# Moving the sixteen tiles of one operand set by 32 bytes each in a two-layer encoder kernel

## The chip, the cores and the metric

The kernel runs on one core of a Trainium2 chip. The metric is the device time of one execution in microseconds, taken over several executions. One further execution was recorded by the hardware profiler; all durations below come from it.

## The reference

The reference is an encoder of two layers on 512 tokens of width 1024, in float32. Layer 0 mixes tokens by dilated sliding-window attention (16 heads, three groups of windows), layer 1 by differential attention (8 heads with two softmaxes each, and a norm on each head's result). Each mixer is followed by a squared-ReLU MLP with 4096 hidden units. Cut to what matters:

```python
for i in range(2):
    hn = rms_norm(h, norm_mix_g[i])
    mix = dilated_window_attention(hn, ...) if i == 0 else differential_attention(hn, ...)
    h = h + mix
    h = h + sq_relu_mlp(rms_norm(h, norm_mlp_g[i]), mlp_w_in[i], mlp_w_out[i])
return rms_norm(h, norm_final_g)

def sq_relu_mlp(xn, w_in, w_out):
    u = jax.nn.relu(xn @ w_in)
    return (u * u) @ w_out
```

## The kernel before, in words

Activations lie transposed: the residual is eight tiles `hT[0..7]` of 128 features by 512 tokens, 2048 bytes in each partition. TensorE multiplies in a short float32 form (`F32R`), so every operand is split into a high part and a low remainder, and every product is three matmuls. The helper `mm3` (L168) issues them in this order: weights high with activations high (L169), weights high with activations low (L170), weights low with activations high (L171).

A matmul here has a stationary operand, loaded by its own instruction (LDWEIGHTS, engine PEld in the profile), and a moving operand that is streamed through. In `linear_steps` (L173) the weights are stationary, 128 columns at a time, and a set of activation tiles is moving, 512 tokens wide. For one block of 128 output features it runs over eight tiles `k` of the set, three matmuls each, so 24 matmuls that accumulate in one PSUM tile. Only in `values1` (L739) it is the other way: there the activations are stationary in slices of 128 tokens, and the weights move, 256 columns wide. The records write a matmul as out<-moving,stationary.

A set of activation tiles is made by `xset` (L128): eight tiles for the high parts and eight for the low parts, each 128 x 512 of four bytes. There are three kinds:

- Set A holds the normed residual. `Norm.feed` (L228) writes a tile of it with one ScalarE instruction (L232, `Ah`) and one VectorE instruction (L233, `Al`). It is the moving operand of all q, k and v products of layer 0, of the q and k products of layer 1 and of all first MLP products, and the stationary operand of `values1`. The norms of both layers, before mixer and MLP, use the same sixteen places in turn.
- Set B (tags `Bh`, `Bl`) holds MLP hidden units; its places also serve for attention operands, and as `oh`, `ol` for the input of the output projections.
- Set C (tags `Ch`, `Cl`, made in `m_in`, not by `xset`) holds the other half of the hidden units.

Weights come in units of 1 MB (`fetch`, L140) through two buffers of three tiles each: `raw`, `whi`, `wlo`, 8192 bytes per partition. ScalarE makes the high part (L158), VectorE the low part (L159).

The order on TensorE is the order in which the program issues, with a few steps woven in (`woven`, L209; hooks in `linear_steps`). Nothing in it depends on where a tile lies.

Where the tiles lie: pools are laid out one behind the other in each partition, in steps of 32 bytes, in the order `const`, `hpool` (the residual, set A, set B), `rpool`, `wpool` (weights), `spool`, and then the pools of a stage. Within `hpool` the order is `h0` to `h7`, `Ah0` to `Ah7`, `Al0` to `Al7`, then the places of set B. In the program before, `Ah0` begins at byte 33888 of each partition, `Al7` at 64608, the first place of set B at 66656, the first `whi` at 121952 and the first `wlo` at 138336. In what follows the **phase** of an operand is its first byte modulo 512. A column block of weights is 128 columns of four bytes, so 512 bytes; a change of `k` or of the block moves it by 1024 or 512 bytes and leaves its phase. The phases before:

| operand | first byte | phase |
|---|---|---|
| `Ah0` to `Al7` | 33888 + 2048 n | 96 |
| set B and its other uses (`oh`, `ol`, `k`, `o`, `pt`) | 66656 + 2048 n | 96 |
| set C, `qh`, `ql`, `nacc`, `h` | various | 96 |
| `whi`, `wlo` | 121952 and on | 96 |
| `ptn`, `psg`, `v0` (layer 0), `p` (layer 1) | 193312 and on | 288 |
| `aT` (layer 1) | 221152, 223200 | 480 |
| `on` (layer 1) | 226336 | 32 |
| `ident` (moving operand of transposes) | 16512 | 128 |

Of the kernel before, what the change touches and what calls it, by code (L numbers as in the profile page):

```python
# [12 lines left out]
F32R = mybir.dt.float32r  # L13
# [6 lines left out]
P = 128  # L20
SEQ = 512
DM = 1024
DFF = 4096
KT = DM // P
# [57 lines left out]
def tile_encoder(ctx: ExitStack, tc: tile.TileContext, x, rel_bias, gains, norm_final_g,  # L82
# [5 lines left out]
    hpool = ctx.enter_context(tc.tile_pool(name="hpool", bufs=1))  # L88
# [37 lines left out]
    hT = [hpool.tile([P, SEQ], F32, tag=f"h{d}", name=f"h{d}") for d in range(KT)]  # L126

    def xset(tag):  # L128
        return ([hpool.tile([P, SEQ], F32R, tag=f"{tag}h{d}", name=f"{tag}h{d}") for d in range(KT)],
                [hpool.tile([P, SEQ], F32R, tag=f"{tag}l{d}", name=f"{tag}l{d}") for d in range(KT)])  # L130

# [86 lines left out]
    class Norm:  # L220


        def __init__(self, gcol, tag):
            self.gcol = gcol
            self.xs = xset(tag) if tag else None
            self.acc = spool.tile([P, SEQ], F32, tag="nacc", name="nacc", bufs=1)
# [368 lines left out]
    for p in range(8):  # L595
        f = sN[:, :, 2 * p:2 * p + 2] if p < 3 else sS[:, :, 2 * p - 6:2 * p - 4]
# [30 lines left out]
    def mlp(i, nm, nxt, last=False):  # L627
# [5 lines left out]
        def m_in(c):  # L633
            if c % 2 == 0:
                hs = xset("B")
            else:
                hs = ([mp.tile([P, SEQ], F32R, tag=f"Ch{d}", name=f"Ch{d}", bufs=1) for d in range(KT)],
                      [mp.tile([P, SEQ], F32R, tag=f"Cl{d}", name=f"Cl{d}", bufs=1) for d in range(KT)])
            chunks[c] = hs

            def on_out(d, ps):
                u = mp.tile([P, SEQ], F32, tag="u", name="u")
                nc.vector.scalar_tensor_tensor(u, ps, 0.0, nm.rB, op0=ALU.max, op1=ALU.mult)  # L643
                nc.scalar.activation(u, u, AF.Square)  # L644
                nc.scalar.copy(hs[0][d], u)
                nc.vector.tensor_sub(hs[1][d], u, f32(hs[0][d]))

            for q in range(4):
                run(linear_steps(2 * q, KT, 256, xs, on_out, bank=wide, hooks=nm.hooks() if c + q == 0 else ()))
# [297 lines left out]
```

## Time and profile before

| | |
|---|---|
| time, median of 3 runs | 1233.21 us (1232.64 to 1233.25) |
| the profiled execution's own time | 1232.82 us |
| its span, first to last instruction | 1231.0 us |
| mean granted TensorE clock | 0.993 |
| VectorE busy | 637.5 us (52%) |
| ScalarE busy | 499.3 us (41%) |
| GpSimd busy | 116.3 us (9%) |
| DMA | 115.73 MB, mean 94 GB/s |

How to read it: the span is what the profile covers, and 1.8 us of the execution's own time lie around it. PE is the matmul engine and PEld its weight loads, which ride beside the matmuls. A matmul's duration runs from its start to a modelled end behind the pipeline, so matmuls of one stream overlap in the records: a 128 x 512 matmul is shown with some 0.39 us, while the next one starts about 0.23 us after it. What a matmul costs is therefore read from the distance between starts; the durations serve to tell one matmul from another. A group row gives line, engine, operation, out<-in, shapes and count, then the busy time in us and the mean of one in ns, then the idle time ahead of it.

### The profile page before, as it was taken

The numbers are of one execution on the slowest core, as the hardware profiler recorded it, in microseconds if no ns is written. First come the engines' busy times: TensorE is split into PE (matmuls) and PEld (weight loads), VectorE is DVE, ScalarE is ACT, GpSimd is POOL, SyncE is SP. The second block draws the span as 40 slices with busy tenths as digits, with TensorE's granted clock in tenths as the row PEclk, the third lists the DMA queues.
The fourth block names the chain that finished last, engine by engine and source line by source line (L and its number), as shares of the span: only waits on it lengthen the run. The fifth ranks groups of instructions, "written<-read, shape, count | busy, mean of one in ns | idle before, by whom it ended". The sixth has DMA issues, their size and how long they took to land.

```text
span 1231.0 us, 15250 instructions
## 1 busy us (share of the span) xinstructions
PE 1206.0 (98%) x6096; PEld 1020.2 (83%) x6096; DVE 637.5 (52%) x1039; ACT 499.3 (41%) x905; POOL 116.3 (9%) x219
## 2 busy tenths in 40 slices
PE   7989999999999999999999999998999999999997
PEld 5778878888888888888888998986888888888897
DVE  7764455645433434434478677673754334344333
ACT  5452433434322323313357667653544223133133
POOL 5000000210000000000201232322300000000012
PEclk9989999999999999999999999998999999999999
DMA  7261222233223333223422333121333223332211
GB/s 226 72 123 56 69 69 69 69 103 103 87 86 102 103 103 102 82 90 103 147 81 87 99 124 104 65 85 52 103 103 102 78 95 103 103 103 99 80 62 69
DMA packets 108307, 115.73 MB, mean 94 GB/s; under 512 B 4507, under 2 KB 101915, under 8 KB 108187
## 3 DMA queue, kind: packets, MB, share of 16 engines
q1 hardware_dynamic: 108236, 114.75, 30.0%
q8 instruction: 48, 0.79, 0.3%
q14 instruction: 23, 0.19, 0.0%
HBM read 112.50 MB, written 2.24 MB: 93 GB/s over the span
## 4 chain that ended last, share of the span: by engine, by line
PE 94%; DVE 2%; DMA 2%; ACT 1%; POOL 0%; issue 0%; SPq 0%; POOLq 0%; DVEq 0%; ACTq 0%
PE acc L169 15%; PE acc L171 15%; PE acc L170 15%; PE s_ps L170 13%; PE s_ps L171 13%; PE s_ps L169 13%; PE o_ps L800 2%; PE s_ps L345 1%; PE s_ps L346 1%; PE t_ps L791 1%; DMA B<-fd 1%; PE o_ps L525 1%; PE s_ps L494 1%; PE o_ps L529 1%; PE t_ps L485 0%; DMA h<-in_x_dram 0%
## 5 line engine op out<-in xcount | busy, mean ns | idle before, releaser
L158 ACT CAST whi<-raw 128x1024 fp32r<-128x1024 f32 (+1 forms) x194 | 192.7, 1039 | 392.8 <-PE s_ps L170 217.1
L159 DVE TENSOR_TENSOR wlo<-raw,whi 128x1024 fp32r<-128x1024 f32 (+1 forms) x194 | 233.7, 1241 | 22.9 <-ACT whi L158 22.5
L171 PE MATMUL acc<-Ah,wlo 128*128 128x512 f32 x472 | 185.9, 394 | 0.0
L169 PE MATMUL acc<-Ah,whi 128*128 128x512 f32 x472 | 185.8, 394 | 0.0
L170 PE MATMUL acc<-Al,whi 128*128 128x512 f32 x472 | 185.7, 393 | 0.0
L169 PE MATMUL s_ps<-Ah,whi 128*128 128x512 f32 x360 | 141.6, 394 | 5.7 <-ACT whi L158 5.5
L170 PE MATMUL s_ps<-Al,whi 128*128 128x512 f32 x360 | 142.1, 395 | 1.8 <-DVE Al L233 1.7
L171 PE MATMUL s_ps<-Ah,wlo 128*128 128x512 f32 x360 | 141.3, 393 | 0.0
L169 PEld LDWEIGHTS acc<-Ah,whi 128*128 128x128 f32 x472 | 89.0, 189 | 18.6 <-ACT sp L338 0.5
L171 PEld LDWEIGHTS acc<-Ah,wlo 128*128 128x128 f32 x472 | 88.8, 188 | 18.7 <-DVE wlo L159 0.5
L170 PEld LDWEIGHTS acc<-Al,whi 128*128 128x128 f32 x472 | 88.9, 188 | 18.1 <-issue 0.5
L169 PEld LDWEIGHTS s_ps<-Ah,whi 128*128 128x128 f32 x360 | 68.2, 190 | 20.3 <-ACT whi L158 5.5
L170 PEld LDWEIGHTS s_ps<-Al,whi 128*128 128x128 f32 x360 | 68.1, 189 | 17.6 <-DVE Al L233 3.8
L171 PEld LDWEIGHTS s_ps<-Ah,wlo 128*128 128x128 f32 x360 | 68.3, 190 | 14.2 <-DVE wlo L159 0.3
L644 ACT ACTIVATE u<-u 128x512 f32<-128x512 f32 x64 | 40.0, 628 | 96.6 <-DVE u L643 95.9
L250 POOL TENSOR_TENSOR nacc<-nacc,nsq 128x512 f32<-128x512 f32 x18 | 27.5, 1529 | 527.1 <-ACT nsq L248 526.6
L653 DVE TENSOR_TENSOR h<-h,s_ps 128x512 f32<-128x512 f32 x33 | 22.7, 688 | 105.4 <-PE s_ps L171 105.4
L643 DVE SCALAR_TENSOR_TENSOR u<-s_ps,rB 128x512 f32<-128x512 f32 x40 | 27.6, 691 | 83.8 <-PE s_ps L171 77.1
L775 DVE CUSTOM_DVE_ANT_0 p<-s_ps,bias 128x512 f32<-128x512 f32 x64 | 43.4, 688 | 31.0 <-PE s_ps L346 20.8
L171 PE MATMUL s_ps<-Bh,wlo 128*128 128x512 f32 x152 | 59.2, 389 | 0.0
L169 PE MATMUL s_ps<-Bh,whi 128*128 128x512 f32 x152 | 59.2, 389 | 0.0
L170 PE MATMUL s_ps<-Bl,whi 128*128 128x512 f32 x152 | 59.1, 389 | 0.0
(237 smaller groups left out, 2269.0 us busy)
## 6 DMA issues: line engine op xcount, KB each, us to landing
raw<-in_mlp_w_in_dram SPq DMA_DIRECT2D x32, 1024.0 KB, 5.3
raw<-in_mlp_w_out_dram SPq DMA_DIRECT2D x32, 1024.0 KB, 5.2
raw<-in_b_w_qkv_dram SPq DMA_DIRECT2D x12, 1024.0 KB, 5.2
raw<-in_a_w_qkv_dram SPq DMA_DIRECT2D x11, 1024.0 KB, 5.2
bias<-fd SPq DMA_DIRECT2D x16, 448.0 KB, 3.6
raw<-in_a_w_o_dram SPq DMA_DIRECT2D x4, 1024.0 KB, 5.2
raw<-in_b_w_o_dram SPq DMA_DIRECT2D x4, 1024.0 KB, 5.2
h<-in_x_dram SPq DMA_DIRECT2D x8, 256.0 KB, 5.1
```

The lines of the kernel that those rows point to most:

```text
L158: nc.scalar.copy(hi[:, k, c], raw[:, k, c])
L159: nc.vector.tensor_sub(lo[:, k, c], raw[:, k, c], f32(hi[:, k, c]))
L169: nc.tensor.matmul(ps, ahi, bhi, start=first, stop=False)
L170: nc.tensor.matmul(ps, ahi, blo, start=False, stop=False)
L171: nc.tensor.matmul(ps, alo, bhi, start=False, stop=last)
L250: eng.tensor_add(self.acc, self.acc, sq)
L345: nc.tensor.matmul(S, q[m][:, qs], k[m][:, ks], start=True, stop=False)
L643: nc.vector.scalar_tensor_tensor(u, ps, 0.0, nm.rB, op0=ALU.max, op1=ALU.mult)
L644: nc.scalar.activation(u, u, AF.Square)
L653: nc.vector.tensor_add(hT[ct], hT[ct], ps)
L775: nc.vector.tensor_tensor_reduce(out=xt, in0=S, in1=bias[h][m][:, b * P:b * P + SEQ], scale=1.0, scalar=3.0e38, op0=ALU.add, op1=ALU.min, ...
L800: marks["PV"] = nc.tensor.matmul(O[:, b, :], aT[:, k, :], v[:, k, es], start=k == 0, stop=k == NB - 1)
```

## The change

Each tile of set A is allocated with 520 columns in place of 512, and only its first 512 columns are handed on. A tile of set A so takes 2080 bytes of each partition, not 2048: `Ah0` stays where it is, each following tile lies 32 bytes further on than before relative to the one ahead of it, and everything behind set A moves by 16 x 32 = 512 bytes. Set B goes through the same helper with its old width. Instructions, their order, shapes and strides within a partition are those of before; only start addresses differ.

```diff
     def xset(tag):
-        return ([hpool.tile([P, SEQ], F32R, tag=f"{tag}h{d}", name=f"{tag}h{d}") for d in range(KT)],
-                [hpool.tile([P, SEQ], F32R, tag=f"{tag}l{d}", name=f"{tag}l{d}") for d in range(KT)])
+
+        n = SEQ + 8 if tag == "A" else SEQ
+        return tuple([hpool.tile([P, n], F32R, tag=f"{tag}{p}{d}", name=f"{tag}{p}{d}")[:, 0:SEQ] for d in range(KT)]
+                     for p in "hl")
```

## The prediction

> **What bounds the kernel now.** I read the page first: how busy each engine is, and who carries the chain of work that ended last.
>
> ```profile
> span 1231.0 us, 15250 instructions
> PE 1206.0 (98%) x6096; PEld 1020.2 (83%) x6096; DVE 637.5 (52%) x1039; ACT 499.3 (41%) x905; POOL 116.3 (9%) x219
> PE 94%; DVE 2%; DMA 2%; ACT 1%; POOL 0%; issue 0%; SPq 0%; POOLq 0%; DVEq 0%; ACTq 0%
> ```
>
> The reader is to see that the matmul engine is busy for 98% of the span and makes 94% of the chain. The table of stretches says the same of a single stage, here the MLP of layer 0 from 230 to 630 us:
>
> ```profile
> 230.00:630.00 400.00, 399.82 (x1787) 331.33 (x1786) 185.24 (x211) 139.21 (x183) 19.39 (x14) 1.00 0.32 101
> ```
>
> Of 400 us the matmul engine is busy for 399.82 (second figure), at the full granted clock (1.00), with VectorE at 185.24 and ScalarE at 139.21. So nothing else is late, and the time is the number of matmuls times the distance between their starts. The change touches neither number of instructions nor order; what it can touch is that distance. Next the groups of matmuls by operands:
>
> ```profile
> L171 PE MATMUL acc<-Ah,wlo 128*128 128x512 f32 x472 | 185.9, 394 | 0.0
> L171 PE MATMUL s_ps<-Ah,wlo 128*128 128x512 f32 x360 | 141.3, 393 | 0.0
> L169 PE MATMUL s_ps<-Bh,whi 128*128 128x512 f32 x152 | 59.2, 389 | 0.0
> L169 PE MATMUL acc<-whi,Ah 128*128 128x256 f32 x128 | 36.5, 285 | 0.0
> ```
>
> Each row has two sisters of the same count (L169, L170 and L171 are the three matmuls of a product). So set A is the moving operand of 3 x 472 + 3 x 360 = 2496 matmuls, and the stationary one of 3 x 128 = 384 narrower ones (last row). That A stands at 394 ns and B at 389 is no property of the tiles: it comes from where the A matmuls stand, as the timelines below show. In the middle of an MLP an A matmul is as quick as any:
>
> ```profile
> 306.04 0.39 PE L171 MATMUL acc<-Ah,wlo 128*128 128x512 f32 x1
> 306.27 0.39 PE L169 MATMUL acc<-Ah,whi 128*128 128x512 f32 x1
> ...
> 308.76 0.39 PE L171 MATMUL acc<-Ah,wlo 128*128 128x512 f32 x1
> 306.27 0.19 PEld L170 LDWEIGHTS acc<-Al,whi 128*128 128x128 f32 x1
> ```
>
> Twelve distances lie between 306.04 and 308.76: 2.72 / 12 = 226.7 ns each. The PEld row shows that the weights of the next matmul are loaded from the moment a matmul starts (306.27 both): the two read the same memory at the same time. That is where the phase could matter.
>
> **What the distance holds.** The granted clock is halved for a few microseconds near 74 us (0.50 in the row of the table of stretches, the last one here), and there 256-wide matmuls stand in a row:
>
> ```profile
> 73.21 0.41 PE L345 MATMUL s_ps<-sp,sp 128*128 128x256 f32 x1
> ...
> 74.28 0.41 PE L346 MATMUL s_ps<-sp,sp 128*128 128x256 f32 x1
> 73.20:74.30 1.10, 1.10 (x8) 1.10 (x7) 1.10 (x2) 1.10 (x4) 0.00 (x0) 0.50 0.72 126
> ```
>
> Five distances in 1.07 us: 214 ns for 256 columns, so 0.836 ns a column at half rate, and half of that, 0.418, at full rate. 512 columns then need 214 ns; the 226.7 ns hold 12.7 ns more, an extra which a slower matrix does not show. I take it for a cost of feeding two operands at once, and 12.7 ns as the most that a better position could give back per matmul. The TensorE page of the Trainium skill ("TensorE: Matmul & The Clock Gate", section "Wait — 56ns, not 53.3ns?") gives a warm matmul of 512 columns 215.7 ns from start to start, that is 2.5 ns of extra; the measured 226.7 ns decides here.
>
> The extra is not fixed. After a few 128-wide instructions the stream needs some ten matmuls to settle:
>
> ```profile
> 659.34 0.40 PE L170 MATMUL acc<-Al,whi 128*128 128x512 f32 x1
> ...
> 660.05 0.39 PE L170 MATMUL acc<-Al,whi 128*128 128x512 f32 x1
> 660.27 0.39 PE L171 MATMUL acc<-Ah,wlo 128*128 128x512 f32 x1
> ...
> 661.43 0.39 PE L170 MATMUL acc<-Al,whi 128*128 128x512 f32 x1
> ```
>
> Nine distances in 2.09 us: 232 ns on average, one of them (660.05 to 660.27) as short as 220 at this view's hundredth of a microsecond. After that the stream is at 227 again. So the distance depends on how the two reads stand against each other in time, settles as long as every matmul is like the last, and is 5.5 ns longer while it searches. How short the short one is, is told by the least of the durations in the view of the tile `Al` (least, median, most):
>
> ```profile
> L170 PE MATMUL acc<-Al,whi x472: 387/389/632, 14.9 to 1125.3; 128*128 128x512 f32 x158
> ```
>
> That is 2 ns under the median. With 256 columns the search goes the other way; in the last product, behind eight transposes:
>
> ```profile
> 1188.11 0.28 PE L170 MATMUL s_ps<-wlo,Ch 128*128 128x256 f32 x1
> ...
> 1188.93 0.28 PE L171 MATMUL s_ps<-whi,Cl 128*128 128x256 f32 x1
> 1189.06 0.28 PE L169 MATMUL s_ps<-whi,Ch 128*128 128x256 f32 x1
> ...
> 1190.26 0.28 PE L170 MATMUL s_ps<-wlo,Ch 128*128 128x256 f32 x1
> ```
>
> Seven distances in 0.82 us while it searches, 117 ns, and ten in 1.20 us when it has settled, 120 ns. A settled stream is not always the quickest.
>
> **Does the position in memory do the same?** Nearly all pairs of moving operand and weights in this kernel have the same phase (96), so the trace shows other phases only at the ends of streams, where the load beside the last matmul is of another tile. Below are rows of narrow windows, each with the last 512-wide matmul of a stream and the one whose operand is loaded beside it; ahead of each stand matmuls of 389 ns, so the stream had settled. First the load of `pt`, then that of `aT`:
>
> ```profile
> L169 PE MATMUL acc<-Ah,whi 128*128 128x512 f32 x1 | 0.4, 389 | 0.0
> L529 PE MATMUL o_ps<-vn,pt 128*128 128x64 f32 x1 | 0.2, 217 | 0.0
> ```
>
> ```profile
> L170 PE MATMUL acc<-Al,whi 128*128 128x512 f32 x1 | 0.4, 397 | 0.0
> L800 PE MATMUL o_ps<-v,aT 128*128 128x128 f32 x1 | 0.3, 274 | 0.0
> ```
>
> Two cases ahead of transposes, with `o` and with `p`:
>
> ```profile
> L169 PE MATMUL s_ps<-oh,whi 128*128 128x512 f32 x1 | 0.4, 393 | 0.0
> L600 PE MATMUL t_ps<-ident,o 128*128 128x128 f32 x1 | 0.3, 270 | 0.0
> ```
>
> ```profile
> L171 PE MATMUL acc<-Ah,wlo 128*128 128x512 f32 x1 | 0.4, 400 | 0.0
> L791 PE MATMUL t_ps<-ident,p 128*128 128x128 f32 x1 | 0.3, 273 | 0.0
> ```
>
> And one with `ptn`, at 106.0 us, ahead of L525:
>
> ```profile
> L169 PE MATMUL acc<-Ah,whi 128*128 128x512 f32 x1 | 0.4, 388 | 0.0
> ```
>
> With `pt` loading (phase 96, like the moving tile) the matmul keeps its 389 ns; with `aT` (phase 480, 384 further) it takes 397. Before transposes, whose load is of another kind, it is 393 with `o` (phase 96) and 400 with `p` (phase 288, 192 further). The last row is the exception: `ptn` is also 192 further, and the matmul stays at 388. So equal phase is the cheapest in both kinds, and another phase costs between 0 and 8 ns. That is thin (few phases, ends of streams), but it is the only evidence on position, and it speaks against the change.
>
> **The change part by part.** It adds and removes no instruction, wait or DMA.
>
> *The 2496 wide matmuls.* `Ah0` keeps its phase; tile n of the sixteen moves to 96 + 32 n, while the weights beside it stay at 96 (512 bytes further for all). So one tile in sixteen keeps the equal phase, and from one matmul to the next the difference jumps by 256 (from `Ah` to `Al` of one k) or by 32 more (to the next k): no matmul is like the last, and the stream may never settle. Bounds per matmul: 0 (the `ptn` row) and +8 ns (the `aT` row); below zero, the 2 ns of the shortest matmuls of the searching stream, and at the very most the 12.7 ns of the extra. I take +4 ns, the middle of 0 and 8, since the perpetual search would give 5.5 and one tile in sixteen pays nothing: 2496 x 4 ns = 10.0 us. All of it lies on the path, as the 399.82 of 400 us show.
>
> *The 384 narrow matmuls of `values1`.* There the weights move and slices of A are loaded, with the same differences. The nearest rows are the searching stream of that width, 3 ns under the settled one, and the wide rows, 0 to 8 ns over: so -1.2 to +3.1 us on 384. I take 0, which lies between, and keep both ends for the range.
>
> *Writing set A.* ScalarE and VectorE write the same 512 contiguous columns. The waits of the matmul engine for them:
>
> ```profile
> PE s_ps L170 <- DVE Al L233: 1.7, 1, 1.7
> ```
>
> One wait of 1.7 us, at the very start; the other writes are hidden behind matmuls. Nothing is taken for this.
>
> *Everything behind set A* moves by 512 bytes, so all phases among B, C, weights and attention tiles are as before: nothing.
>
> The sum: 1232.82 us (the profiled execution: span 1231.0 and 1.8 around it) + 10.0 = 1242.8. The median of the runs shown, 1233.21, is 0.4 above the profiled one, so 1243.2. Its own range is +2 to +8 ns per matmul, 5 to 20 us: 1238 to 1253.
>
> **The rivals.**
>
> *No effect.* The position plays no part; what differs at the ends of streams is the kind of the following instruction, and the 232 ns of the searching stream are a matter of time alone. For it: the `ptn` row, and the fact that matmuls of sets A and B settle at the same 389. Against it: 389 and 397 for loads of one kind and width, 393 and 400 for the other. The time would be 1233.2. Here belongs too that the change might not do what it says, if tiles were laid out in coarser steps than 32 bytes; single-column tiles of 4 bytes lie 32 apart, so I give that 0.02. The Trainium skill ("SBUF — State Buffer", section "Who interferes with whom") states that TensorE has two independent read ports, for the moving operand and for the weights, and never waits on anyone: by that rule the sum is 1233.2 too. The trace does not fit it well: two loads of 128 columns each, beside the same kind of matmul, left 389 and 397 ns.
>
> *Faster: equal phase is the bad case.* If matmul and load meet in the same place because they start at the same phase, then spreading the phases removes meetings. For it: an extra of 12.7 ns stands in every wide matmul, all at equal phase, and searching streams dip under the settled value, by 2 ns in single wide matmuls and by 3 ns on average in narrow ones. Against it: in the five cases above no other phase is under 388. The point from which it decides is a mean distance over the sixteen tiles under 226.7 ns; at 2 ns less it is 2496 x 2 = 5.0 us, with the 1.2 us of the narrow ones 6.2, so 1227.0 from the median. The full 12.7 ns would be 31.7 us, 1201.5; I see no row that gets near that.
>
> **How the numbers follow.** Slower as forecast: 0.60. No effect, the skill's rule and the layout case included: 0.22. Faster: 0.18, most of it between 1227 and the edge of no change. About 0.2%, 2.5 us, is what a measurement of this kernel can tell from no change: faster is under 1230.7, slower over 1235.7. The range that should hold 8 in 10 goes from 1227 (the faster case) to 1256 (8 ns on all wide matmuls is 1253.2, and most of the 3.1 us of the narrow ones on top); about 0.08 is left out at each end.
>
> **What would show it.** In the profile after, the groups `acc<-Ah`, `acc<-Al` and their `s_ps` sisters rise from 393 to 395 ns to about 398, the B rows stay at 389, the stretch 230 to 630 grows by some 4 ns for each A matmul in it, and a timeline of an MLP's first product shows no constant 226.7 ns, but a pattern that repeats with the eight tiles. It is wrong if the A groups stay within 1 ns (no effect), if they fall (equal phase was the bad case), or if B rows change too, since then the 512 bytes of shift matter and the phase modulo 512 is not the right measure.

## The result, and the profile after

The changed kernel takes 1244.38 us (median of 4 runs, 1243.79 to 1245.76) against 1233.23 us (4 runs, 1232.64 to 1233.97): a ratio of 1.0092, with a 95% interval of 1.0074 to 1.0109. It is slower by 11.15 us. The profiled execution has a span of 1242.0 us, 11.0 more than before. Line numbers from the changed helper on are higher by two (L169 is now L171).

The page, the lines that answer to those shown of before:

```profile
span 1242.0 us, 15250 instructions
PE 1216.9 (98%) x6096; PEld 1018.7 (82%) x6096; DVE 637.4 (51%) x1039; ACT 499.5 (40%) x905; POOL 116.3 (9%) x219
PE 95%; DMA 2%; DVE 1%; ACT 1%; POOL 0%; SPq 0%; issue 0%; POOLq 0%; DVEq 0%; ACTq 0%
```

The number of instructions is the same, and so, nearly, is the busy time of the other engines: VectorE 637.4 for 637.5, ScalarE 499.5 for 499.3, GpSimd 116.3 in both, the weight loads 1018.7 for 1020.2. Only the matmul engine is busier, by 10.9 us. The table of stretches, the MLP of layer 0:

```profile
230.00:630.00 400.00, 399.82 (x1758) 327.03 (x1757) 179.59 (x202) 133.55 (x174) 19.38 (x14) 1.00 0.31 101
```

In the same 400 us the engine is as busy as before, but gets through 1758 matmuls, not 1787. No wait was added; each matmul takes longer. Which ones, the groups of the page tell:

```profile
L173 PE MATMUL acc<-Ah,wlo 128*128 128x512 f32 x472 | 188.1, 399 | 0.0
L171 PE MATMUL acc<-Ah,whi 128*128 128x512 f32 x472 | 188.1, 398 | 0.0
L172 PE MATMUL acc<-Al,whi 128*128 128x512 f32 x472 | 187.1, 396 | 0.0
L171 PE MATMUL s_ps<-Ah,whi 128*128 128x512 f32 x360 | 143.5, 399 | 5.6 <-ACT whi L160 5.6
L172 PE MATMUL s_ps<-Al,whi 128*128 128x512 f32 x360 | 143.1, 398 | 2.5 <-DVE Al L235 2.4
L173 PE MATMUL s_ps<-Ah,wlo 128*128 128x512 f32 x360 | 143.2, 398 | 0.0
```

These six groups are busy for 993.1 us together, where before they had 982.4 (185.9 + 185.8 + 185.7 + 141.6 + 142.1 + 141.3): 10.7 us, or 4.3 ns for each of the 2496 matmuls. The wait for `Al` has grown from 1.7 to 2.4 us, still a single one at the start. The same view by operand shapes gives the neighbours:

```profile
L171 PE MATMUL s_ps<-Bh,whi 128*128 128x512 f32 x152 | 59.2, 389 | 0.0
L171 PE MATMUL acc<-whi,Ah 128*128 128x256 f32 x128 | 36.3, 284 | 0.0
```

Set B, which moved together with the weights, is at 389 ns as before. The narrow matmuls with set A stationary are not slower but a little faster (284 for 285 ns, and its sisters 283 and 282).

The timeline of an MLP's first product no longer shows one distance:

```profile
300.37 0.39 PE L172 MATMUL acc<-Al,whi 128*128 128x512 f32 x1
300.60 0.40 PE L173 MATMUL acc<-Ah,wlo 128*128 128x512 f32 x1
300.83 0.40 PE L171 MATMUL acc<-Ah,whi 128*128 128x512 f32 x1
301.07 0.39 PE L172 MATMUL acc<-Al,whi 128*128 128x512 f32 x1
...
305.95 0.39 PE L172 MATMUL s_ps<-Al,whi 128*128 128x512 f32 x1
```

From 300.37 to 305.95 lie 24 distances, once round the eight tiles with three matmuls each: 5.58 us, 232.5 ns on average, where it was 226.7. The durations go between 0.39 and 0.40 from one matmul to the next. In the trace's own start times, which are finer than this view, the distances repeat with every 24 matmuls, as forecast.

### The profile page after: what moved, and what is told of

The parts are those of the page before. It is cut to its first block, busy times and chain, and to the rows that moved or that the text cites. A ratio compares the mean times of both kernels' runs of the same rounds, so it can differ in the third digit from the quotient of the medians.

```text
span 1242.0 us, 15250 instructions
## 1 busy us (share of the span) xinstructions
PE 1216.9 (98%) x6096; PEld 1018.7 (82%) x6096; DVE 637.4 (51%) x1039; ACT 499.5 (40%) x905; POOL 116.3 (9%) x219
## 4 chain that ended last, share of the span: by engine, by line
PE 95%; DMA 2%; DVE 1%; ACT 1%; POOL 0%; SPq 0%; issue 0%; POOLq 0%; DVEq 0%; ACTq 0%
PE acc L171 15%; PE acc L173 15%; PE acc L172 15%; PE s_ps L173 13%; PE s_ps L172 13%; PE s_ps L171 13%; PE o_ps L802 2%; PE s_ps L347 1%; PE s_ps L348 1%; PE t_ps L793 1%; DMA B<-fd 1%; PE o_ps L527 1%; PE s_ps L496 1%; PE o_ps L531 1%; PE t_ps L487 0%; DMA h<-in_x_dram 0%
## 5 line engine op out<-in xcount | busy, mean ns | idle before, releaser
L171 PE MATMUL acc<-Ah,whi 128*128 128x512 f32 x472 | 188.1, 398 | 0.0
L172 PE MATMUL acc<-Al,whi 128*128 128x512 f32 x472 | 187.1, 396 | 0.0
L171 PE MATMUL s_ps<-Ah,whi 128*128 128x512 f32 x360 | 143.5, 399 | 5.6 <-ACT whi L160 5.6
L172 PE MATMUL s_ps<-Al,whi 128*128 128x512 f32 x360 | 143.1, 398 | 2.5 <-DVE Al L235 2.4
L172 PEld LDWEIGHTS acc<-Al,whi 128*128 128x128 f32 x472 | 88.9, 188 | 20.3 <-issue 0.5
L171 PEld LDWEIGHTS acc<-Ah,whi 128*128 128x128 f32 x472 | 88.9, 188 | 20.2 <-ACT sp L340 0.5
L171 PEld LDWEIGHTS s_ps<-Ah,whi 128*128 128x128 f32 x360 | 68.0, 189 | 21.7 <-ACT whi L160 5.6
L172 PEld LDWEIGHTS s_ps<-Al,whi 128*128 128x128 f32 x360 | 68.1, 189 | 20.2 <-DVE Al L235 4.2
L171 PE MATMUL s_ps<-Bh,whi 128*128 128x512 f32 x152 | 59.2, 389 | 0.0
L172 PE MATMUL s_ps<-Bl,whi 128*128 128x512 f32 x152 | 59.2, 389 | 0.0
```

Source lines behind the costliest of these rows:

```text
L171: nc.tensor.matmul(ps, ahi, bhi, start=first, stop=False)
L172: nc.tensor.matmul(ps, ahi, blo, start=False, stop=False)
```

## Theories

The prediction put two things into one price: that a position other than the equal one costs something by itself, and that jumping positions keep the stream from settling. The experiments take them apart.

- **Theory S**: the variation costs. Any constant position settles at 226.7 ns.
- **Theory P**: the position costs. A constant shift of all of set A costs as much, and a single odd tile costs only at its own matmuls.
- Besides: is it the position of set A by itself, or against the weights (**theory W**)? And by which distance does it repeat?

All shifts below are made with pads behind tiles, at most 512 bytes in all (1024 where the weights are moved), and instructions and their order are those of before.

## Experiments on set A: which shift costs

The edit is a helper with a pad behind each tile, for example for the shift of all tiles by 32 bytes (`u32`):

```diff
-    hT = [hpool.tile([P, SEQ], F32, tag=f"h{d}", name=f"h{d}") for d in range(KT)]
+    hT = [hpool.tile([P, SEQ + (8 if d == 7 else 0)], F32, tag=f"h{d}", name=f"h{d}")[:, 0:SEQ] for d in range(KT)]
...
+    PAD = {"h": [0, 0, 0, 0, 0, 0, 0, 0], "l": [0, 0, 0, 0, 0, 0, 0, 120]}
...
+            n = SEQ + (PAD[p][d] if tag == "A" else 0)
+            return hpool.tile([P, n], F32R, tag=f"{tag}{p}{d}", name=f"{tag}{p}{d}")[:, 0:SEQ]
```

The others differ only in the pads (in elements of four bytes): `u256` has 64 behind the residual and 64 behind `Al7`, `lo256` has 64 behind `Ah7` and 64 behind `Al7`, `one32` has 8 behind `Ah2` and 120 behind `Ah3`; `u64`, `u128`, `u192`, `u224` are like `u32` with that many bytes. In these kernels the three lines of `mm3` are L170 to L172, one higher than before.

All tiles 32 bytes further (`u32`):

> All sixteen tiles of set A lie 32 bytes further against the weights, all by the same amount (a pad behind the last residual tile, the rest of 512 bytes behind Al7). Theory S (what costs is that the position varies from matmul to matmul, so that the stream never settles): it settles at 226.7 ns as before, the A groups stay at 393 to 395 ns, 1232 to 1235 us. Theory P (equal phase is good, any other position costs): all 2496 wide matmuls pay 2 to 8 ns, 1238 to 1253 us.

Measured: 1246.72 us against 1232.76, ratio 1.0108 (1.0093 to 1.0123). Theory S falls. The timeline:

```profile
300.07 0.39 PE L172 MATMUL acc<-Ah,wlo 128*128 128x512 f32 x1
300.30 0.40 PE L170 MATMUL acc<-Ah,whi 128*128 128x512 f32 x1
300.54 0.39 PE L171 MATMUL acc<-Al,whi 128*128 128x512 f32 x1
...
304.27 0.39 PE L172 MATMUL s_ps<-Ah,wlo 128*128 128x512 f32 x1
```

Eighteen distances in 4.20 us are 233.3 ns. The stream is constant in its operands' positions, and still does not come down to 226.7.

All tiles 256 bytes further (`u256`):

> All sixteen tiles of set A lie 256 bytes further against the weights, all by the same amount. Theory S: settles, 1232 to 1235 us. Theory P: 1238 to 1253 us; if P holds by the size of the difference, another time than with 32 bytes.

Measured: 1232.74 us, ratio 1.0002 (0.9992 to 1.0012). No change; S and P would both be served by this one if the position repeats every 256 bytes.

Only the low tiles 256 bytes further (`lo256`):

> The eight high tiles stay, the eight low tiles lie 256 bytes further: in each group of three matmuls the middle one differs. Theory S: a pattern of period three that may not settle, the A groups near those of the changed kernel (396 to 399 ns), 1239 to 1245 us. Theory P: only the 832 matmuls with a low tile pay 2 to 8 ns, 1235 to 1240 us, and the L169 and L171 groups stay at 394.

Measured: 1232.93 us, ratio 1.0000 (0.9991 to 1.0010). Both expectations miss: neither a price of the position nor one of the variation. Together with `u256` it says that 256 bytes are the same position.

One tile 32 bytes further (`one32`):

> Only Ah3 lies 32 bytes further; the other fifteen tiles keep the equal phase. Theory S: two odd matmuls in each 24 start a search of some ten matmuls, so about half of the loss of the changed kernel, 1236 to 1241 us. Theory P: 208 matmuls pay 2 to 8 ns, 0.4 to 1.7 us, 1233 to 1235 us.

Measured: 1234.05 us, ratio 1.0010 (1.0001 to 1.0019): 1.3 us, what theory P said. The timeline shows the odd tile and what follows:

```profile
302.19 0.39 PE L172 MATMUL s_ps<-Ah,wlo 128*128 128x512 f32 x1
302.42 0.40 PE L170 MATMUL s_ps<-Ah,whi 128*128 128x512 f32 x1
302.65 0.39 PE L171 MATMUL s_ps<-Al,whi 128*128 128x512 f32 x1
302.88 0.39 PE L172 MATMUL s_ps<-Ah,wlo 128*128 128x512 f32 x1
303.12 0.39 PE L170 MATMUL s_ps<-Ah,whi 128*128 128x512 f32 x1
303.34 0.39 PE L171 MATMUL s_ps<-Al,whi 128*128 128x512 f32 x1
```

The distances that begin at 302.42, 302.65 and 302.88 are 230, 230 and 240 ns at this view's hundredth of a microsecond, and that at 303.12 is 220; a settled 226.7 is shown by this view as 230 or 220. So a disturbed stream finds its way in about four matmuls here, not ten, and the disturbance itself is cheap.

The other constant shifts tell by which distance the position repeats.

> All of set A 64 bytes further against the weights. Position counts modulo 64: 1232 to 1235 us. Modulo 128 or 256: slower, by as much as with 32 bytes (12 to 15 us) if any unequal position costs the same, by another amount if the price follows the size of the difference.

> All of set A 128 bytes further. Position counts modulo 64 or 128: 1232 to 1235 us. Modulo 256: slower, 1238 to 1250 us.

> All of set A 192 bytes further. Modulo 64: 1232 to 1235 us. Modulo 128: the time of the 64-byte kernel. Modulo 256: a time of its own. The load of ptn, 192 bytes off, left its matmul at 388 ns before, which speaks for no change here and so for modulo 64; the load of p, 192 off as well, stood beside 400 ns, which speaks for slower.

> All of set A 224 bytes further, which modulo 256 is 32 bytes back. If only the distance counts, the time of the 32-byte kernel, 1244 to 1248 us. If it counts which of the two reads is ahead, another time; faster than before is possible only here, as the one position at which the moving read trails the load.

Times against the kernel before on the same chip, and the mean distance of 18 starts in the first MLP product (first start near 300 us):

| shift of all of set A, bytes | mean distance, ns | time, us | before, us | ratio (95%) |
|---|---|---|---|---|
| 0 | 226.7 | | | 1 |
| 32 | 233.3 | 1246.72 | 1232.76 | 1.0108 (1.0093 to 1.0123) |
| 64 | 228.9 | 1236.95 | 1233.30 | 1.0028 (1.0016 to 1.0040) |
| 128 | 233.3 | 1246.27 | 1233.30 | 1.0107 (1.0090 to 1.0124) |
| 192 | 233.3 | 1245.71 | 1233.30 | 1.0102 (1.0087 to 1.0117) |
| 224 | 232.8 | 1245.40 | 1233.30 | 1.0101 (1.0086 to 1.0116) |
| 256 | 226.7 | 1232.74 | 1232.76 | 1.0002 (0.9992 to 1.0012) |

At the view's hundredth of a microsecond a mean over 18 distances is good to some 0.6 ns, so 232.8 is no other value than 233.3. A longer stretch of the same MLP counts the matmuls in 150 us (the number behind the second figure); the rows are those of the table in its order, 0 to 256 bytes, and the last is `lo256`:

```profile
275.00:425.00 150.00, 150.00 (x663) 124.25 (x662) 65.66 (x78) 52.11 (x68) 0.00 (x0) 1.00 0.29 94
275.00:425.00 150.00, 150.00 (x650) 121.55 (x649) 63.47 (x75) 51.17 (x68) 0.00 (x0) 1.00 0.30 95
275.00:425.00 150.00, 150.00 (x659) 123.38 (x658) 66.07 (x78) 52.14 (x69) 0.00 (x0) 1.00 0.29 92
275.00:425.00 150.00, 150.00 (x650) 121.67 (x649) 63.19 (x76) 51.22 (x69) 0.00 (x0) 1.00 0.30 95
275.00:425.00 150.00, 150.00 (x650) 121.68 (x649) 63.98 (x76) 51.16 (x68) 0.00 (x0) 1.00 0.30 97
275.00:425.00 150.00, 150.00 (x650) 121.73 (x649) 63.72 (x76) 51.18 (x68) 0.00 (x0) 1.00 0.29 92
275.00:425.00 150.00, 150.00 (x663) 124.21 (x662) 65.91 (x78) 52.11 (x68) 0.00 (x0) 1.00 0.29 93
275.00:425.00 150.00, 150.00 (x664) 124.20 (x662) 65.40 (x77) 52.32 (x69) 0.00 (x0) 1.00 0.30 96
```

The shifts by 32, 128, 192 and 224 bytes give one and the same count, 650, at the full granted clock. So the price does not grow with the difference. Neither 64 nor 128 bytes are a period; 256 is the least shift tried that changes nothing. It also counts which operand is ahead: modulo 256, a shift by 192 bytes is one by 64 bytes back, and it pays 6.6 ns where 64 bytes on pay 2.2. The 64-byte kernel has this middle price in its timeline:

```profile
300.32 0.39 PE L170 MATMUL s_ps<-Ah,whi 128*128 128x512 f32 x1
300.55 0.39 PE L171 MATMUL s_ps<-Al,whi 128*128 128x512 f32 x1
300.78 0.39 PE L172 MATMUL s_ps<-Ah,wlo 128*128 128x512 f32 x1
301.01 0.39 PE L170 MATMUL s_ps<-Ah,whi 128*128 128x512 f32 x1
...
302.38 0.39 PE L170 MATMUL s_ps<-Ah,whi 128*128 128x512 f32 x1
```

Nine distances in 2.06 us are 228.9 ns. By lines, from 300.5 to 304.0 us, each of the three matmuls of a product has its own duration, so the stream repeats in groups of three:

```profile
L171 PE MATMUL s_ps<-Al,whi 128*128 128x512 f32 x6 | 2.4, 394 | 0.0
L170 PE MATMUL s_ps<-Ah,whi 128*128 128x512 f32 x6 | 2.4, 392 | 0.0
L172 PE MATMUL s_ps<-Ah,wlo 128*128 128x512 f32 x5 | 1.9, 388 | 0.0
```

No position tried gives a wide stream a shorter distance than the equal one. In all kernels of the table but the one with 256 bytes the narrow matmuls of `values1` were faster; for the 224-byte kernel, by shapes:

```profile
L170 PE MATMUL acc<-whi,Ah 128*128 128x256 f32 x128 | 36.1, 282 | 0.0
L172 PE MATMUL acc<-whi,Al 128*128 128x256 f32 x128 | 36.0, 281 | 0.0
```

These are 282 and 281 ns where the kernel before has 285: for narrow products the equal position is not the best.

## Experiments on the weights

To see whether it is the position against the weights, set A was left alone and the weights were moved within larger tiles (`w32`; `w16` has 4 in place of 8):

```diff
-        hi = wpool.tile([P, kt, ncol], F32R, tag="whi", name="whi")
-        lo = wpool.tile([P, kt, ncol], F32R, tag="wlo", name="wlo")
+        off = 8
+        hi, lo = (wpool.tile([P, kt * ncol + 64], F32R, tag=t, name=t)[:, off:off + kt * ncol]
+                  .rearrange("p (k c) -> p k c", k=kt) for t in ("whi", "wlo"))
...
-                    sq = mp.tile([P, 256], F32, tag="sqN", name="sqN")
+                    sq = mp.tile([P, 256], F32, tag="sqN", name="sqN", bufs=1)
...
-            sq = l1p.tile([P, P], F32, tag="sq", name="sq")
+            sq = l1p.tile([P, P], F32, tag="sq", name="sq", bufs=1)
```

Weights 32 bytes later (`w32`):

> No tile of set A moves; the split weights begin 32 bytes later in their tiles (each made 256 bytes larger; two scratch tiles that nobody reads have one buffer instead of two to make room). Theory W (what counts is moving operand against weights): all 4224 wide products pay, those of sets B and C too, whose groups rise from 389 to 393 to 396 ns; 6.6 ns each as with set A 32 bytes back, 28 us, less 2 us at the narrow ones: 1255 to 1262 us. Theory A (something about where set A itself lies): no change, 1232 to 1235 us, B and C at 389.

Measured: 1254.01 us against 1233.01, ratio 1.0176 (1.0160 to 1.0193); 21 us, where 22 to 29 were expected, so theory W holds with a price a little under the expected one. Sets B and C did not move and pay now, by the same view as above:

```profile
L170 PE MATMUL s_ps<-Bh,whi 128*128 128x512 f32 x152 | 60.1, 396 | 0.0
L170 PE MATMUL s_ps<-Ch,whi 128*128 128x512 f32 x112 | 44.3, 396 | 0.0
```

Both are at 396 where they were at 389. So it is the moving operand's position against the weights that are loaded beside it. The larger tiles and the scratch tiles are not the cause, since `nar32` below has them too and its wide streams stay at 663 matmuls in 150 us.

A second sign is that weights 32 bytes later and set A 32 bytes back (`u224`) are the same difference. Two matmuls of each, first `u224`, then `w32`:

```profile
300.23 0.40 PE L172 MATMUL acc<-Ah,wlo 128*128 128x512 f32 x1
300.46 0.40 PE L170 MATMUL acc<-Ah,whi 128*128 128x512 f32 x1
300.15 0.40 PE L171 MATMUL acc<-Al,whi 128*128 128x512 f32 x1
300.38 0.40 PE L172 MATMUL acc<-Ah,wlo 128*128 128x512 f32 x1
```

In both timelines every matmul from 300.3 to 304.5 us is shown with 0.40 us, while `u32`, with set A 32 bytes on, goes between 0.39 and 0.40 at the same mean distance. No run moved both operands by the same amount, which would be the direct test.

Weights 16 bytes later (`w16`):

> As before, with the weights 16 bytes later in place of 32. If the price is one of any unequal position, 1255 to 1262 us. If there is a step of 32 bytes under which position counts for nothing, 1232 to 1235 us. A time under 1230 us would be a better position than the equal one.

Measured: nine runs from 1233.04 to 1254.16 us, median 1244.31, which none of the expectations has; only the lowest runs fit the second one. They lie in three heaps: three at 1233.0 to 1234.2, four at 1243.3 to 1246.6, two at 1253.5 and 1254.2. The mean granted clock of the nine lies between 0.991 and 0.995 and does not follow the heaps (0.994 at 1254.16 us, 0.992 at 1234.13), so it does not set them apart. The profiled execution, with a span of 1232.4 us, was of the lowest heap. Its stretches within the MLPs of the two layers:

```profile
275.00:425.00 150.00, 150.00 (x663) 124.28 (x662) 66.06 (x79) 53.82 (x72) 0.00 (x0) 1.00 0.30 97
900.00:1150.00 250.00, 250.00 (x1105) 207.07 (x1104) 104.17 (x120) 79.67 (x102) 0.00 (x0) 1.00 0.30 97
```

The same kernel once more, for a second profile (`w16b`):

> The kernel with the weights 16 bytes later once more, for a second profile. If its streams can settle in two ways, a slower execution shows whole streams at about 233 ns from start to start (B and C groups near 396 ns), and one between shows both kinds side by side; if something else made its times scatter, the wide groups stay at 389 and the lost time stands in a wait.

Measured: 1243.35 us, span 1241.6, this time of the middle heap:

```profile
275.00:425.00 150.00, 150.00 (x645) 121.47 (x644) 62.87 (x74) 50.46 (x67) 0.00 (x0) 1.00 0.29 94
900.00:1150.00 250.00, 250.00 (x1104) 207.01 (x1104) 107.69 (x126) 83.78 (x110) 0.00 (x0) 1.00 0.30 96
```

In the MLP of layer 0 the engine gets through 645 matmuls in 150 us, not 663; in that of layer 1 it has 1104 in 250 us, as in the first profile (`w32`, slow in both, has 645 and 1074). The program is the same, and the granted clock is 1.00 in all four rows. So with 16 bytes of difference a stream can settle in either of two ways, 233 or 227 ns, and keeps it through a whole MLP. One MLP in the slower way costs some 10 us (the two profiled spans differ by 9.2), which would give the three heaps: none, one, or both. Only the lowest and the middle heap were profiled; that both MLPs are slow in the highest is argued from its time. What decides at the start of a stream was not tried.

**A version that beats both.** The table says that wide products want equal positions, and the rows of `values1` that narrow ones do not. `values1` is not the only place where the weights move: in the last product of layer 1 they do so too, with set C stationary, so there are twice 384 narrow matmuls. Only the weights of these two (`nar32`) are moved by 32 bytes, with the larger tiles and the two scratch tiles as in `w32`; `w_last` stands for the second MLP weights of layer 1:

```diff
+        off = 8 if (w is b_w_qkv and c0 >= 2 * DM) or (w is w_last and r0 == 3 * 1024) else 0
```

> Only the weights of the narrow products (values1, and the last MLP product of layer 1) begin 32 bytes later; all wide products keep equal positions. Theory W with a better position for narrow products: the 768 narrow matmuls go from 119.8 to about 117 ns from start to start, 2 us less, 1230.5 to 1231.5 us, wide groups unchanged. If the narrow gain in the earlier kernels came only from the unsettled wide streams ahead of them: no change, 1232.5 to 1234 us.

Measured: 1230.43 us (11 runs, 1229.61 to 1231.88) against 1233.01, ratio 0.9978 (0.9969 to 0.9987). It is 2.6 us faster than before, as theory W said, and 14 us faster than the changed kernel. Its last product:

```profile
1185.05 0.28 PE L171 MATMUL s_ps<-whi,Ch 128*128 128x256 f32 x1
1185.17 0.28 PE L172 MATMUL s_ps<-wlo,Ch 128*128 128x256 f32 x1
...
1186.33 0.28 PE L173 MATMUL s_ps<-whi,Cl 128*128 128x256 f32 x1
```

Eleven distances in 1.28 us are 116.4 ns, and the stream stays there where it settled at 120 before. On 768 narrow matmuls 3.6 ns would be 2.8 us; it is a little less in truth, since some of them, behind other work, stood near 117 ns before.

## Why the prediction was right, point by point

- *The bound*: right. The matmul engine carries 95% of the chain, no other engine's work grew, and all of the loss stands in the distance between matmuls.
- *The 2496 wide matmuls at +4 ns, 10.0 us*: the term came out at 4.3 ns and 10.7 us by the six groups. Of the bounds, the one read from the load of `aT`, +8 ns, is a good guess of the price: that load lies 384 bytes further, which modulo 256 is 128, and the 128-byte kernel pays 233.3 - 226.7 = 6.6 ns.
- *The reason given for taking half of it* did not hold. The prediction said that no matmul is like the last and the stream may never settle. `u32` has constant positions and pays more (233.3 ns) than the changed kernel (232.5), and `one32` shows that a single jump is over in a few matmuls. So the term came out near its size in part by luck. What lowers the price from 6.6 to 4.3 is, as far as the runs show, an average over positions, and that many A matmuls do not stand in a settled stream: even `u32` loses only 13.96 us, 5.6 ns on each of the 2496, where its settled streams lose 6.6. A rough check: the changed kernel's tiles go through 0, 32, 64 and on to 224 bytes, for high and low tiles alike modulo 256. The six of these eight positions that were measured alone have a mean of 231.4 ns, against 232.5 in the changed kernel, so some 1 ns is left for the jumping itself, if the two positions that were not measured (96 and 160 bytes) cost as much as the mean.
- *The phase modulo 512*: too long a period. It is 256, so two of the sixteen tiles (`Ah0`, `Al0`) kept the equal position, not one.
- *The `ptn` row*, taken as a sign that 192 bytes may cost nothing: the load there lies 192 bytes further than the moving tile, so the moving tile is, modulo 256, 64 bytes ahead of the load. The constant shift that answers to it is thus that of the 64-byte kernel, which costs 2.2 ns, and not that of `u192`, as the expectation for that run took it. The load of `p` has the same difference, and its matmul stood at 400 ns, 7 over that beside `o`. A single matmul behind a stream that had settled elsewhere is a weak witness.
- *The 384 narrow matmuls, taken as 0 between -1.2 and +3.1 us*: they fell, by 0.8 us (36.5 + 36.5 + 36.4 before, 36.3 + 36.2 + 36.1 after).
- *Set B and what lies behind set A*: unchanged at 389 ns, as said.
- *No effect*: `w32` decides against it, since two operands that only changed their distance cost 21 us. The Trainium skill ("SBUF — State Buffer", section "Who interferes with whom") gives TensorE two independent read ports and says that it never waits on anyone; by that rule the 21 us would be none, and the measurement decides.
- *Equal phase is the bad case*: wrong for wide matmuls at all positions tried, right for narrow ones.

The dependence on the difference modulo 256 bytes is measured; what makes it is open. That both reads meet in the same part of the memory is a picture that fits it; which part of the chip this is, the runs don't show. Nor do they show why 64 bytes cost less than 32 or 128, or why four shifts cost the same.

## What to carry to other kernels

In a kernel that is bound by matmuls, the start addresses of the moving operand and of the weights loaded beside it are worth a look: here equal positions modulo 256 bytes gave 226.7 ns per 512-wide matmul, others up to 233.3, while 256-wide ones did better 32 bytes apart, 117 against 120 ns. Tiles whose sizes are multiples of 256 bytes keep equal positions equal, if their pools begin so; a pad that looks harmless, for whatever reason it is put there, can cost 1%. The ends of streams, where another tile is loaded, hint in the old trace that an unequal position costs something, but not how much: the readings there went from -1 to +8 ns, where constant shifts cost 2.2 or 6.6.

## What the runs showed that was not expected

- At 16 bytes of difference the same program had times from 1233.0 to 1254.2 us, and in the two profiles streams that settled at 227 or 233 ns stayed there for a whole MLP.
- At constant positions the streams settle in short cycles: the 64-byte kernel repeats every three matmuls, and its mean of 228.9 ns lies well under the 233.3 of its neighbours at 32 and 128 bytes.
